# Three-block kernel with eight experts: 42 weight units multiplied whole in fp32, and a reordering of routing, row transposes and multiplications

## The chip, the cores and the metric

One Trainium2 chip, one core of it. The metric is the device time of one execution in microseconds (us). The kernel before was run three times: median 1424.33 us, from 1423.22 to 1425.75. The profile was taken of one more execution.

## What is computed

One sequence of 256 tokens with 1024 channels passes a gated-delta mixer, a SwiGLU block, a sliding-window attention block and a mixture of eight experts, each followed by a residual and a layer norm, all in fp32. The change lies in the last of them:

```python
def moe_swiglu(x, w_router, w_gate, w_up, w_down):
    bsz, t, d = x.shape
    xf = x.reshape(bsz * t, d)
    logits = (xf @ w_router).astype(jnp.float32)
    top_val, top_idx = lax.top_k(logits, TOP_K)
    top_w = jax.nn.softmax(top_val, axis=-1)
    gates = jnp.einsum('nk,nke->ne', top_w, jax.nn.one_hot(top_idx, N_EXPERTS, dtype=jnp.float32))
    out = jnp.zeros_like(xf)
    for e in range(N_EXPERTS):
        h = jax.nn.silu(xf @ w_gate[e]) * (xf @ w_up[e])
        out = out + gates[:, e:e + 1].astype(xf.dtype) * (h @ w_down[e])
    return out.reshape(bsz, t, d)
```

Each token takes two of the eight experts. Gate and up weights are 1024 x 3584 per expert, down weights 3584 x 1024: 44 MB of weights per expert, 352 MB in all.

## The kernel before, in words

**Units and the ring.** Expert weights arrive in units of 1 MB (128 partitions x 2048 fp32). An expert has 42: 14 for gate, 14 for up, 14 for down. SyncE (SP) issues their DMAs in the order of use, into a ring of ten tiles named `raw` (three of `ring_a`, two of `ring_m`, and five tiles of earlier stages); two of the ten leave the ring in the last expert, for the tiles `y` and `lngb`. A tile is free again once nothing reads it any more.

**Splitting.** `unit` (L141) makes two fp32r parts of a unit: `hi`, a cast on ScalarE (ACT, L154), and `lo = raw - hi`, a subtraction on VectorE (DVE, L155). Both have four buffers, so a split can be four units ahead of the multiplication.

**Heavy and light experts.** The rows of an expert's tokens, at most 128, are gathered to `xr`, transposed (L1139) and split into `xg` (high and low part). In `arms` (L1172) TensorE (PE) branches on the number of tokens. Above 64 the expert is *heavy*: `mm3` (L165) multiplies three times for each chunk of 128 channels and 512 columns (high x `hi`, low x `hi`, high x `lo`; L170, L171, L173). At or below 64 it is *light*: `packed` (L1109) has put 64 columns of the high part and 64 of the low part side by side into `xp`, and `mm2` (L1192) needs two products (L1195); `addlow` (L1184) then adds the lower half of the result to the upper one, by a product with `fold`. A unit has four chunk-and-column pairs, so it takes 12 products in a heavy expert and 8 in a light one. With the inputs used here the lines in the trace show experts 0, 2, 3 and 5 heavy, and 1, 4, 6 and 7 light. Expert 0 always takes the heavy path and gathers its rows by products (L1127) instead.

**The order of an expert.** Columns are taken in blocks `b` of 512, in pairs (0,1), (2,3), (4,5) and a single 6. The list `stages` runs, for a pair, gate of both, up of both, down of the *previous* pair, then a stage `held`. For a pair the even `b` holds channels 0 to 511 of both column blocks and the odd `b` channels 512 to 1023, two units each. `held` (from L1352) folds the up result and multiplies it with the activated gate: `V.tensor_mul(s_, s_, pu)` (L1355), tile `msg`. `turn_one` then transposes a `msg` (L1243) for the down products. `keep` stores an expert's result in `ys` at block 2 of the next expert.

**Routing.** After the last layer norm, `route` ranks the logits, `gates` (L1032) makes the softmax weights, and `places` (L1064) makes the row `key` of each token, on GpSimd (POOL) with reductions on DVE. Four indirect DMAs on POOL's queue (L1168) scatter the token rows to `xs`; `fetch` (L1117) loads one expert's rows to `xr`. `gather(e + 1)` is called behind the up stage of block 3 of expert `e`.

**Who sets the order.** The instructions of a stage are placed by a scheduler of the framework, not by the text alone; `tc.issue_after(i)` holds instructions back until `i` has been placed.

Of the kernel before, what the change touches and what calls it, by code (L numbers as in the profile page):

```python
# [30 lines left out]
P = 128  # L31
# [51 lines left out]
def kernel(ctx: ExitStack, tc: tile.TileContext, A, out):  # L83
# [73 lines left out]

    def colunits(w, c0, n):
# [8 lines left out]
    def mm3(ps, xh, xl, whs, first, last):  # L167
# [4 lines left out]
        for k, (_, wl) in enumerate(whs):  # L172
            PE.matmul(ps, xh(k), wl, start=False, stop=last and k == n - 1)  # L173
# [836 lines left out]
    def route(tb, plg, done):  # L1010
# [3 lines left out]
        gt_, eq_ = (rt.tile(sq, F32, name=n + str(tb)) for n in ("gt", "eq"))  # L1014
# [69 lines left out]
    with ExitStack() as mctx:  # L1084
# [36 lines left out]
        def gather(e):  # L1121
# [7 lines left out]

            if e == 0:  # L1130
                for k in range(KC):
                    pick(k, 0)
            for g in range(2):
                p = pg[g] if e == 0 else trb()
                for k in range(4 * g, 4 * g + 4):
                    if e == 0:
                        pick(k, 1)
                    else:
                        PE.transpose(p[:, k % 4 * P:(k % 4 + 1) * P], xr[e][:, k * P:(k + 1) * P], ident)  # L1139
# [7 lines left out]
        xg, xp = {}, {}  # L1147
# [14 lines left out]
        with tc.issue_after(placed.ins):  # L1162
            for tb in range(2):
                gates(tb, lgs[tb])
# [32 lines left out]
        def gateup(e, b, us, ps, then=lambda: None):  # L1197
# [4 lines left out]

            def parts():
# [284 lines left out]
```

## Time and profile before

| what | value |
|---|---|
| median of three runs | 1424.33 us |
| the profiled execution's own time | 1427.08 us |
| its span in the profile | 1425.4 us |
| PE, DVE, ACT busy | 1314.1, 1165.6, 1012.1 us |
| DMA bytes | 446.76 MB |
| first product of expert 0 | 475.2 us |

Each later expert is cut off where POOL stores the result of the one before it (the `ys` DMA, L1260): 634.80, 743.96, 868.56, 988.09, 1097.51, 1217.34 and 1325.01 us. Such a stretch begins in block 2 of an expert and ends in block 2 of the next, so it holds 34 units of one expert and 8 of the next.

How to read it: "busy" counts the time in which an engine has an instruction under way; PE's ends are modelled, so that its busy time also holds the drain of the last product before a gap. "Idle before" a group names what ended the wait. SPq, POOLq and PEq are the queues ahead of these engines. A PE product of fp32r operands has one record in the trace; one of fp32 operands has two.

### The profile page before, as it was taken

How to read it: one execution, taken by the hardware profiler on the slowest of the kernel's cores; microseconds unless marked ns; L12 is line 12 of the kernel's file. 1: busy time of each engine (PE TensorE's matmuls, PEld its weight loads, DVE VectorE, ACT ScalarE, POOL GpSimd, SP SyncE). 2: the span in 40 equal slices, each digit the busy share in tenths (PEclk: the TensorE clock that was granted, in tenths of full speed). 3: DMA queues.
4: the chain of work that ended last, by engine and by line, in shares of the span. 5: the costliest groups of instructions: out<-in, count | busy, mean ns of one | idle time of the engine just before them, and what ended most of it. 6: DMA issues, size and time to landing. Idle time of an engine off the chain costs nothing. (4 is left out here: it accounts for less than half of the span.)

```text
span 1425.4 us, 17392 instructions
## 1 busy us (share of the span) xinstructions
PE 1314.1 (92%) x6175; PEld 1046.2 (73%) x6175; DVE 1165.6 (82%) x1293; ACT 1012.1 (71%) x1264; POOL 68.0 (5%) x97
## 2 busy tenths in 40 slices
PE   7999999999898969988899999999889999888884
PEld 5888788888777858866677777776667777666663
DVE  4885975554878768889998887889999888999998
ACT  4764544443364657689888878779988888998983
POOL 4000000000000310000000000000000000002110
PEclk9999999999999889999999999999999999999997
DMA  8641577653644899999999999999999999999992
GB/s 283 208 125 60 178 271 237 229 207 120 226 148 170 307 366 336 362 368 392 419 413 380 367 358 368 376 343 408 413 420 411 377 369 374 396 414 416 419 416 87
DMA packets 145378, 446.76 MB, mean 313 GB/s; under 512 B 12704, under 2 KB 20032, under 8 KB 145264
## 3 DMA queue, kind: packets, MB, share of 16 engines
q1 hardware_dynamic: 137072, 420.64, 77.8%
q0 software_dynamic: 5280, 18.66, 3.5%
q10 hardware_dynamic: 2912, 5.90, 1.2%
q8 instruction: 76, 1.25, 0.3%
q14 instruction: 38, 0.31, 0.1%
HBM read 435.05 MB, written 15.36 MB: 316 GB/s over the span
## 5 line engine op out<-in xcount | busy, mean ns | idle before, releaser
L155 DVE TENSOR_TENSOR lo<-raw,hi 128x2048 fp32r<-128x2048 f32 (+1 forms) x610 | 910.3, 1532 | 119.1 <-ACT hi L154 109.2
L154 ACT CAST hi<-raw 128x2048 fp32r<-128x2048 f32 (+1 forms) x610 | 768.4, 1310 | 156.5 <-PE acc L171 61.3
L1195 PE MATMUL acc<-lo,xp 128*128 128x512 f32 x224 | 76.8, 431 | 22.3 <-DVE lo L155 20.1
L170 PE MATMUL acc<-hi,hT 128*128 128x512 f32 x224 | 89.1, 398 | 2.0 <-ACT hi L154 2.0
L170 PE MATMUL mm<-hi,xg 128*128 128x512 f32 x224 | 87.8, 393 | 0.5 <-ACT low L1189 0.5
L170 PE MATMUL acc<-hi,xg 128*128 128x512 f32 x224 | 87.8, 392 | 0.0
L171 PE MATMUL acc<-hi,hT 128*128 128x512 f32 x224 | 87.8, 392 | 0.0
L171 PE MATMUL mm<-hi,xg 128*128 128x512 f32 x224 | 87.4, 390 | 0.0
L171 PE MATMUL acc<-hi,xg 128*128 128x512 f32 x224 | 87.2, 389 | 0.0
L1195 PE MATMUL mm<-lo,xp 128*128 128x512 f32 x224 | 70.8, 403 | 9.6 <-DVE lo L155 9.4
L1195 PEld LDWEIGHTS acc<-lo,xp 128*128 128x128 f32 x224 | 39.6, 195 | 50.4 <-DVE lo L155 44.5
L1195 PE MATMUL acc<-lo,hp 128*128 128x512 f32 x224 | 71.5, 400 | 3.4 <-DVE lo L155 3.4
L1195 PE MATMUL acc<-hi,hp 128*128 128x512 f32 x224 | 70.8, 397 | 1.2 <-ACT hp L1115 1.2
L1195 PE MATMUL mm<-hi,xp 128*128 128x512 f32 x224 | 68.9, 394 | 2.2 <-ACT low L1189 1.5
L1195 PE MATMUL acc<-hi,xp 128*128 128x512 f32 x224 | 70.7, 403 | 0.0
L173 PE MATMUL acc<-lo,hT 128*128 128x512 f32 x224 | 69.4, 391 | 0.0
L173 PE MATMUL mm<-lo,xg 128*128 128x512 f32 x224 | 67.7, 389 | 0.0
L173 PE MATMUL acc<-lo,xg 128*128 128x512 f32 x224 | 67.7, 389 | 0.0
L1355 DVE TENSOR_TENSOR msg<-msg,acc 128x512 f32<-128x512 f32 x56 | 36.4, 681 | 36.5 <-PEq L1179 33.3
L1195 PEld LDWEIGHTS mm<-lo,xp 128*128 128x128 f32 x224 | 40.2, 188 | 26.8 <-DVE lo L155 19.4
L1114 ACT CAST hp<-tr 128x256 fp32r<-128x256 f32 x49 | 18.6, 380 | 54.7 <-DVE hT L1247 54.7
L1243 PE MATMUL tr<-ident,msg 128*128 128x128 f32 x224 | 34.9, 284 | 22.5 <-DVE msg L1355 22.5
(411 smaller groups left out, 2326.3 us busy)
## 6 DMA issues: line engine op xcount, KB each, us to landing
raw<-in_moe_w_gate_dram SPq DMA_DIRECT2D x112, 1024.0 KB, 7.6
raw<-in_moe_w_up_dram SPq DMA_DIRECT2D x112, 1024.0 KB, 7.5
raw<-in_moe_w_down_dram SPq DMA_DIRECT2D x112, 1024.0 KB, 7.9
raw<-in_a_w_in_dram SPq DMA_DIRECT2D x12, 1024.0 KB, 5.3
raw<-in_ffn_w_gate_dram SPq DMA_DIRECT2D x11, 1024.0 KB, 5.1
raw<-in_ffn_w_up_dram SPq DMA_DIRECT2D x11, 1024.0 KB, 5.0
raw<-in_ffn_w_down_dram SPq DMA_DIRECT2D x11, 1024.0 KB, 4.9
raw<-in_b_w_in_dram SPq DMA_DIRECT2D x5, 1024.0 KB, 5.0
```

Of the source, the lines that this page charges most:

```text
L154: S.copy(hi[:, c], raw[:, c])
L155: subs.append(V.tensor_sub(lo[:, c], raw[:, c], hi[:, c].bitcast(F32)))
L170: PE.matmul(ps, xh(k), wh, start=first and k == 0, stop=False)
L171: PE.matmul(ps, xl(k), wh, start=False, stop=False)
L173: PE.matmul(ps, xh(k), wl, start=False, stop=last and k == n - 1)
L1114: S.copy(v[:, :, 0], p)
L1195: PE.matmul(ps, x[:, (k0 + i % n) * P:(k0 + i % n + 1) * P], w, start=first and i == 0, stop=last and i == 2 * n - 1)
L1243: PE.transpose(p[:, f * P:(f + 1) * P], s[:, f * P:(f + 1) * P], ident)
L1355: V.tensor_mul(s_, s_, pu)
```

## The change

It does four things. (1) `as_is` loads a unit without splitting it. `loads` uses it in experts 1 to 7 for the second unit of the odd blocks 1, 3 and 5, of gate and of up (channels 768 to 1023): six units of an expert, 42 in all. `whole_part` multiplies such a unit directly, four products of fp32 operands for either path, with `xf`, a plain fp32 copy of the last two chunks of the transposed rows, which ACT makes once per expert. (2) `places` now runs ahead of `gates`, on DVE, and the scatters are issued ahead of `gates`; what weights the pairs is a function of its own, `pair_gates`. (3) `gather(1)` moves from block 3 to block 5 of expert 0, and its transposes are held until the products just recorded are placed. (4) The multiplication leaves `held` for the next pair's first gate stage, except behind blocks 5 and the last one.

```diff
+    def as_is(src, a, b):
+        raw = next(raws[0])()[:, :a * b].rearrange("p (a b) -> p a b", a=a)
+        nc.sync.dma_start(raw, src)
+        return raw
...
-            PE.matmul(ps, xh(k), wl, start=False, stop=last and k == n - 1)
+            turn[0] = PE.matmul(ps, xh(k), wl, start=False, stop=last and k == n - 1)
...
-        row, spill, one, val = (rt.tile(sq, F32, name=n) for n in ("row", "spill", "one", "val"))
-        G.tensor_tensor(row, pos, place[:, None, :E].to_broadcast(sq), op=OP.add)
-        G.tensor_tensor(spill, place[:, E:, None].to_broadcast(sq), row, op=OP.subtract)
-        G.tensor_scalar(val, pos, float(P), None, op0=OP.is_ge)
-        G.tensor_tensor(spill, spill, val, op=OP.mult)
-        G.tensor_tensor(row, row, spill, op=OP.add)
+        row, spill, val = (rt.tile(sq, F32, name=n) for n in ("row", "spill", "val"))
         key = rt.tile([P, 2, 2], F32, name="key")
+        V.tensor_tensor(row, pos, place[:, None, :E].to_broadcast(sq), op=OP.add)
+        V.tensor_tensor(spill, place[:, E:, None].to_broadcast(sq), row, op=OP.subtract)
+        V.scalar_tensor_tensor(spill, pos, float(P), spill, op0=OP.is_ge, op1=OP.mult)
+        V.tensor_add(row, row, spill)
         for j in range(2):
-            G.tensor_scalar(one, rank, float(j), None, op0=OP.is_equal)
-            for src, dst in ((row, key), (gate, gat2)):
-                G.tensor_tensor(val, one, src, op=OP.mult)
-                V.tensor_reduce(dst[:, j], val, axis=AX.X, op=OP.add)
-        V.tensor_copy(keyi, key)
+            V.scalar_tensor_tensor(val, rank, float(j), row, op0=OP.is_equal, op1=OP.mult)
+            V.tensor_reduce(key[:, j], val, axis=AX.X, op=OP.add)
+            V.tensor_copy(keyi[:, j], key[:, j])
...
+            late = ExitStack()
...
+            elif e == 1:
+                late.enter_context(tc.issue_after(turn[0].ins))
...
+                if g and e:
+                    xf[e] = mp.tile([P, 2 * P], F32, name="xf", tag="xf")
+                    S.copy(xf[e], p[:, 2 * P:])
...
         with tc.issue_after(placed.ins):
-            for tb in range(2):
-                gates(tb, lgs[tb])
             places()
...
+        with tc.issue_after(placed.ins):
+            for tb in range(2):
+                gates(tb, lgs[tb])
+            pair_gates()
...
+            def whole_part(ws):
+                for h, p in enumerate(ps):
+                    for k in range(2):
+                        PE.matmul(p, xf[e][:, k * P:(k + 1) * P], ws[:, k, h * 512:(h + 1) * 512], start=False, stop=k == 1)
...
                 for u, ws in enumerate(us):
+                    if not isinstance(ws, tuple):
+                        whole_part(ws)
+                        continue
...
-            return [unit(v[:, k0 + 2 * u:k0 + 2 * u + 2, c0:c0 + 1024], 2, 1024) for u in range(2)]
+            return [(as_is if e and k0 + 2 * u == KC - 2 else unit)(
+                v[:, k0 + 2 * u:k0 + 2 * u + 2, c0:c0 + 1024], 2, 1024) for u in range(2)]
...
+        def multiply():
+            for bb, pu, _, s_, ee in mine:
+                V.tensor_mul(s_, s_, pu)
+                held.append((ee, bb, s_))
+            mine.clear()
...
-                if held:
+                if b % 2 == 0 and b < NB - 1:
+                    multiply()
+                elif held:
                     turn_one()
...
-                if b == 3 and e + 1 < NE:
+                if b == 5 - 2 * (e > 0) and e + 1 < NE:
                     xg[e + 1] = gather(e + 1)
...
-                for bb, pu, _, s_ in mine:
-                    V.tensor_mul(s_, s_, pu)
-                    held.append((e, bb, s_))
-                mine.clear()
+                if b == NB - 2 or (e, b) == (NE - 1, NB - 1):
+                    multiply()
```

Where the scheduler puts this shows at three places. The first is PE in expert 0, behind the up products of block 3 (before) and of block 5 (now); `xr` holds the fetched rows of expert 1, `hT` the transposed `msg` for the down products, and `tr` is a PSUM bank. Before:

```order
1513 L170 MATMUL acc<-hi,xg 128x512
1514 L171 MATMUL acc<-hi,xg 128x512
1515 L173 MATMUL acc<-lo,xg 128x512 x2
1516 L1139 MATMUL tr<-ident,xr 128x128 x8
1517 L170 MATMUL acc<-hi,hT 128x512
```

Now, at the new place:

```order
1635 L175 MATMUL acc<-hi,xg 128x512
1636 L176 MATMUL acc<-hi,xg 128x512
1637 L178 MATMUL acc<-lo,xg 128x512 x2
1638 L1152 MATMUL tr<-ident,xr 128x128 x8
1639 L175 MATMUL acc<-hi,hT 128x512
```

The eight transposes moved back by 122 rows of PE's order, past the down products of blocks 0 and 1 and the gate and up products of blocks 4 and 5.

The second place is PE in a gate stage of an odd block of a later expert: the heavy path, a branch, the light path. `mm` is the gate's PSUM bank. Now:

```order
2703 L175 MATMUL mm<-hi,xg 128x512
2704 L176 MATMUL mm<-hi,xg 128x512
2705 L178 MATMUL mm<-lo,xg 128x512 x2
2706 L1224 MATMUL mm<-raw,xf 128x512 x4
2707 L1197 UNCONDITIONAL_BRANCH
2708 L1213 MATMUL mm<-hi,xp 128x512 x2
2709 L1213 MATMUL mm<-lo,xp 128x512 x2
2710 L1213 MATMUL mm<-hi,xp 128x512 x2
2711 L1213 MATMUL mm<-lo,xp 128x512 x2
2712 L1224 MATMUL mm<-raw,xf 128x512 x4
2713 L1197 UNCONDITIONAL_BRANCH
```

Before, the second half of either path was the first one over again; now four products read `raw` itself, in both paths.

The third place is DVE about the multiplications of a pair (`msg`), in expert 3. Before:

```order
721 L155 TENSOR_TENSOR lo<-raw,hi 128x2048
722 L1179 UNCONDITIONAL_BRANCH
723 L1355 TENSOR_TENSOR msg<-msg,acc 128x512 x2
724 L155 TENSOR_TENSOR lo<-raw,hi 128x2048
725 L1179 UNCONDITIONAL_BRANCH
726 L155 TENSOR_TENSOR lo<-raw,hi 128x2048
727 L1247 TENSOR_TENSOR hT<-tr,hT 128x512
```

Now:

```order
718 L155 TENSOR_TENSOR lo<-raw,hi 128x2048
719 L1197 UNCONDITIONAL_BRANCH
720 L1346 TENSOR_TENSOR msg<-msg,acc 128x512 x2
721 L155 TENSOR_TENSOR lo<-raw,hi 128x2048
722 L1197 UNCONDITIONAL_BRANCH
723 L155 TENSOR_TENSOR lo<-raw,hi 128x2048
724 L1273 TENSOR_TENSOR hT<-tr,hT 128x512
```

Between the down units' splits nothing moved: the multiplications stand where they stood, although the text calls them one stage later.

## Rows read from the trace of the kernel before

**Rows 1.** The page: span.

```profile
span 1425.4 us, 17392 instructions
```

**Rows 2.** Windows: stretches of experts 1, 2, 4 and 6, cut at the result DMAs.

```profile
core 0: us, PE busy (x) PEld busy (x) DVE busy (x) ACT busy (x) POOL busy (x), PEclk, DMA share, GB/s
634.80:744.00 109.20, 97.57 (x417) 73.00 (x416) 103.38 (x60) 99.29 (x98) 1.11 (x3) 1.00 1.02 408
744.00:868.60 124.60, 120.30 (x543) 98.19 (x542) 103.91 (x59) 99.84 (x95) 1.06 (x3) 1.00 0.97 367
988.10:1097.50 109.40, 97.69 (x416) 73.20 (x415) 103.35 (x59) 98.70 (x95) 1.06 (x2) 1.00 1.03 416
1217.30:1325.00 107.70, 93.80 (x388) 67.15 (x387) 104.22 (x59) 98.40 (x95) 8.98 (x7) 1.00 1.02 409
```

**Rows 3.** Timeline of PE in expert 0 (start, us, line, tiles, wait in brackets).

```profile
519.43 0.61 PE L173 MATMUL acc<-lo,xg 128*128 128x512 f32 x2
530.82 1.94 PE L1139 MATMUL tr<-ident,xr 128*128 128x128 f32 x8 [10.78 <-DMA xr<-xs]
```

**Rows 4.** Windows behind that wait; columns as in rows 2.

```profile
531.00:534.00 3.00, 3.00 (x12) 2.71 (x12) 1.28 (x2) 1.79 (x4) 0.55 (x1) 0.50 0.00 1
534.00:537.00 3.00, 3.00 (x12) 2.36 (x11) 2.52 (x6) 2.25 (x7) 0.00 (x0) 0.80 0.53 175
```

**Rows 5.** Timeline of POOL: the first scatter, the first fetch.

```profile
481.63 1.29 POOL L1168 DMA_INDIRECT xs<-x,keyi  x1 [0.58 <-DVE keyi L1079]
...
523.85 0.59 POOL L1119 DMA_DIRECT2D xr<-xs  x1 [7.31 <-issue]
```

**Rows 6.** Timeline of PE in expert 2, fp32r products.

```profile
774.76 0.39 PE L170 MATMUL mm<-hi,xg 128*128 128x512 f32 x1
...
777.48 0.39 PE L170 MATMUL mm<-hi,xg 128*128 128x512 f32 x1
```

**Rows 7.** Timeline of PE in the attention, fp32 products of 256 columns.

```profile
412.40 1.13 PE L890 MATMUL mm<-akT,aqT 64*128 64x256 f32 x4
413.46 0.50 PE L178 MATMUL acc<-hi,aTh 128*128 128x512 f32 x1
```

**Rows 8.** The same, fp32 products of 128 columns.

```profile
384.78 1.16 PE L890 MATMUL mm<-akT,aqT 64*128 64x128 f32 x8
385.86 0.39 PE L178 MATMUL mm<-hi,x2Th 128*128 128x256 f32 x1
```

**Rows 9.** Groups by form, stretch of expert 6 (busy us, mean ns, idle before).

```profile
L155 DVE TENSOR_TENSOR lo<-raw,hi 128x2048 fp32r<-128x2048 f32 x43 | 97.6, 2311 | 3.6 <-ACT hi L154 3.3
L154 ACT CAST hi<-raw 128x2048 fp32r<-128x2048 f32 x42 | 79.0, 1931 | 0.0
```

**Rows 10.** Timeline of PE in expert 2, about the transposes of a pair.

```profile
766.62 0.61 PE L173 MATMUL acc<-lo,hT 128*128 128x512 f32 x2
768.18 1.25 PE L1243 MATMUL tr<-ident,msg 128*128 128x128 f32 x8 [0.94 <-DVE msg L1355]
```

**Rows 11.** Waits of SP, same stretch (us in total, times, longest).

```profile
SPq L145 <- DVE lo L155: 89.7, 40, 4.5
```

**Rows 12.** DMA issues in that stretch (KB each, median us to landing).

```profile
raw<-in_moe_w_down_dram SPq DMA_DIRECT2D x13, 1024.0 KB, 8.0
```

**Rows 13.** Windows of 25 us in expert 7; columns as in rows 2.

```profile
1340.00:1365.00 25.00, 21.90 (x91) 15.44 (x90) 24.30 (x15) 22.42 (x21) 0.00 (x0) 1.00 1.02 420
```

**Rows 14.** DMA issues in expert 7, from 1335 to 1390 us.

```profile
raw<-in_moe_w_down_dram SPq DMA_DIRECT2D x10, 1024.0 KB, 13.2
```

**Rows 15.** Windows at the end; columns as in rows 2.

```profile
1390.00:1395.00 5.00, 5.00 (x18) 3.80 (x18) 5.00 (x7) 3.22 (x5) 0.00 (x0) 0.81 0.90 367
1400.00:1405.00 5.00, 3.83 (x17) 2.81 (x17) 5.00 (x4) 2.10 (x3) 0.00 (x0) 1.00 0.00 0
```

More of the change, by code (lines that the diff above doesn't have):

```diff
@@ L1013, in route @@
         sq = [P, E, E]
-        gt_, eq_ = (rt.tile(sq, F32, name=n + str(tb)) for n in ("gt", "eq"))
+        gt_, eq_ = (rt.tile(sq, F32, name=n, tag=n) for n in ("gt", "eq"))
         le, lo_ = lg[:, :, None].to_broadcast(sq), lg[:, None, :].to_broadcast(sq)
@@ L1066, in places, with pair_gates @@
         sq = [P, 2, E]
-        row, spill, one, val = (rt.tile(sq, F32, name=n) for n in ("row", "spill", "one", "val"))
-        G.tensor_tensor(row, pos, place[:, None, :E].to_broadcast(sq), op=OP.add)
-        G.tensor_tensor(spill, place[:, E:, None].to_broadcast(sq), row, op=OP.subtract)
-        G.tensor_scalar(val, pos, float(P), None, op0=OP.is_ge)
-        G.tensor_tensor(spill, spill, val, op=OP.mult)
-        G.tensor_tensor(row, row, spill, op=OP.add)
+        row, spill, val = (rt.tile(sq, F32, name=n) for n in ("row", "spill", "val"))
         key = rt.tile([P, 2, 2], F32, name="key")
+        V.tensor_tensor(row, pos, place[:, None, :E].to_broadcast(sq), op=OP.add)
+        V.tensor_tensor(spill, place[:, E:, None].to_broadcast(sq), row, op=OP.subtract)
+        V.scalar_tensor_tensor(spill, pos, float(P), spill, op0=OP.is_ge, op1=OP.mult)
+        V.tensor_add(row, row, spill)
         for j in range(2):
-            G.tensor_scalar(one, rank, float(j), None, op0=OP.is_equal)
-            for src, dst in ((row, key), (gate, gat2)):
-                G.tensor_tensor(val, one, src, op=OP.mult)
-                V.tensor_reduce(dst[:, j], val, axis=AX.X, op=OP.add)
-        V.tensor_copy(keyi, key)
+            V.scalar_tensor_tensor(val, rank, float(j), row, op0=OP.is_equal, op1=OP.mult)
+            V.tensor_reduce(key[:, j], val, axis=AX.X, op=OP.add)
+            V.tensor_copy(keyi[:, j], key[:, j])
+    def pair_gates():
+        val = rt.tile([P, 2, E], F32, name="gval")
+        for j in range(2):
+            G.tensor_scalar(val, rank, float(j), None, op0=OP.is_equal)
+            G.tensor_tensor(val, val, gate, op=OP.mult)
+            V.tensor_reduce(gat2[:, j], val, axis=AX.X, op=OP.add)
     def at(j, tb):
@@ L1132, in gather @@
                     pick(k, 0)
+            elif e == 1:
+                late.enter_context(tc.issue_after(turn[0].ins))
             for g in range(2):
                 p = pg[g] if e == 0 else trb()
[L1135 to L1139, printed above, removed]
+                with late.pop_all():
+                    for k in range(4 * g, 4 * g + 4):
+                        if e == 0:
+                            pick(k, 1)
+                        else:
+                            PE.transpose(p[:, k % 4 * P:(k % 4 + 1) * P], xr[e][:, k * P:(k + 1) * P], ident)
                 hi, lo = (xg[:, n, 4 * g:4 * g + 4, :].rearrange("p a c -> p (a c)") for n in range(2))
@@ L1345 @@
                         S.activation(s_, pg, AF.Silu)
-                        mine.append((b - len(pgs) + 1 + n, pu, low(pu) if e else None, s_))
+                        mine.append((b - len(pgs) + 1 + n, pu, low(pu) if e else None, s_, e))
                 if b == 1 and e + 1 < NE:
                     fetch(e + 1)
-                if b == 3 and e + 1 < NE:
+                if b == 5 - 2 * (e > 0) and e + 1 < NE:
                     xg[e + 1] = gather(e + 1)
@@ L1352 @@
                 if e:
-                    arms(e, lambda: None, lambda: [addlow(pu, lu_) for _, pu, lu_, _ in mine])
-                for bb, pu, _, s_ in mine:
-                    V.tensor_mul(s_, s_, pu)
-                    held.append((e, bb, s_))
-                mine.clear()
+                    arms(e, lambda: None, lambda: [addlow(pu, lu_) for _, pu, lu_, _, _ in mine])
+                if b == NB - 2 or (e, b) == (NE - 1, NB - 1):
+                    multiply()
                 if (e, b) == (NE - 1, NB - 1):
```

2 lines of the change are left out of this document (1 added, 1 removed).

## The prediction

> **What bounds the kernel now.** The page's span is 1425.4 us [rows 1]; the execution it shows took 1427.08 us, 2.75 us more than the median of the runs, 1424.33. The sum below is made against 1427.08 and its difference is then taken from the median. About 2.8 us, 0.2%, is what a measurement of this kernel can tell from no change.
>
> I read the expert stage by windows first, cut where an expert's result leaves. Two kinds of stretch appear [rows 2]. In heavy expert 2 PE is busy for 120.30 of 124.60 us, DVE and ACT for 104 and 100: PE is the bound. In light experts 1, 4 and 6 (109.2, 109.4, 107.7 us) DVE is busy for 103 to 104 us and PE for 94 to 98: DVE is the bound, with ACT (98 to 99) close behind. A share averaged over the kernel hides this: what helps a light expert, less splitting, costs a heavy one if PE has to do more.
>
> Data is not far off. DMA moves 408 to 416 GB/s in the light stretches [rows 2] and never much over the 420 GB/s of expert 7 [rows 13]. Still it is not what a light expert waits for: SP, which issues the loads, waits 40 times and 89.7 us for a subtraction of DVE to free a ring tile, and for nothing else [rows 11]. The ring thus runs full. Ten tiles of 2.56 us (107.7 / 42) are 25.6 us from issue to release; 8.0 us of that is the transfer [rows 12] and 4.2 us the cast and the subtraction (1.93 and 2.31 us, [rows 9]). So some 13 us, five tiles, lie landed and wait. In expert 7, with eight tiles, a transfer takes 13.2 us from issue to landing [rows 14] at 420 GB/s: there DMA is the bound, until the last load has landed at about 1395 us. From 1400 to 1405 us DVE is still busy throughout [rows 15].
>
> The one long wait of PE in this stage is in expert 0: 10.78 us at the transposes of expert 1's rows, for the fetch of `xr` [rows 3], which POOL could issue only at 523.85 us, behind four scatters, the first of them at 481.63 [rows 5]. The clock granted to PE is 0.50 in the 3 us behind it, the lower of its two levels (1.2 of 2.4 GHz), and 0.80 on average in the next three [rows 4]; ahead of that PE had stood for those 10.78 us.
>
> **The change part by part.**
>
> *Transposes later, keys first.* The order puts the eight transposes behind the up products of block 5. PE needs them there some 60 us later than now, and the rows come earlier, since nothing of the softmax stands ahead of the first scatter any more. The wait goes, 10.8 us, and so does the slow clock behind it: half of 3 us and a fifth of 3 us, 2.1 us. PE has no other idle time there that could swallow it. Gain 12.9 us; I allow 9 to 13, since the same eight transposes now delay the down products of block 2. What is late next is PE itself. The ten or so small instructions of the keys, moved from POOL to DVE, I take at nothing: DVE's splits are ahead of PE there, and without that cover they would cost some 2 us. `pair_gates` on POOL now stands between the first and the second scatter; nobody waits for those until block 5.
>
> *Whole units in the heavy experts 2, 3 and 5.* 18 units lose a cast and a subtraction, on engines that are not the bound: worth nothing. On PE twelve fp32r products leave: from 774.76 to 777.48 are twelve, 2.72 us [rows 6]. Four fp32 products of 512 columns come, eight records; no row has that shape. The nearest: four records of 256 columns take 1.06 us to the next product [rows 7], eight of 128 columns 1.08 us [rows 8]. Taking 2 columns' time at 2.4 GHz for each column, 0.107 and 0.213 us a record, both leave about 0.2 us that a group costs once. With 0.427 and 0.01 us a record and 0.19 a group, a unit takes 3.68 us, 0.96 more than now. Bounds: 3.41 us (no cost but the columns) and 4.20 us (0.525 a record, the straight line through the two rows). 18 units: **+17.3 us**, from +12.4 to +26.6. I take the middle value since it fits both rows.
>
> *Whole units in the light experts.* Each loses six casts and six subtractions: DVE falls from 104.2 to 90.3 us, ACT from 98.4 to about 87, one small copy for `xf` not counted. PE gains: now 336 products and 16 folds at 0.227 us and 36 transposes at 0.13 (eight are issued in 1.0 of the 1.25 us of [rows 10]) are 84.6 us; six units change 8 products (1.82 us) for 3.68, so +11.2. At each of four `held` stages PE also stands for 1.1 us, from 767.08, when the last product has been fed, to 768.18, when the first `msg` is there [rows 10]. Together 100.2 us: PE becomes the longest of the three. The gain of an expert is then at most 107.7 - 100.2 = 7.5 us. Data needs 42 units of 1.049 MB and 1.05 MB for rows and results, 45.1 MB; at 420 GB/s [rows 13] this is 107.4 us. A light expert can beat that only out of the tiles that lie ready: 7.2 us are three tiles of five. Experts 1 and 4 stand alone between heavy ones, in which the ring fills again (367 GB/s is all that expert 2 takes, [rows 2]). I take 5.5 us each, three quarters, because PE will meet a late split now and then; bounds 0 and 7.5.
>
> The Trainium skill ("DMA: Bandwidth & Descriptors", Specifications and "Where 436 GB/s comes from") speaks against any gain here: it says that loads from HBM are held to about 358 GB/s for a core, with 435 as the ceiling of the fabric. The rows stand at 408 to 420 and disagree with the first. By 358 a light expert would need an estimated 126 us and the terms of all light experts would be nought, the sum +4.4; by 435 data would need an estimated 103.7 us and those terms would reach the bounds of PE.
>
> *Experts 6 and 7* follow each other, so the tiles in hand count once. What DMA can still gain is the 409 of 420 GB/s of expert 6, 2.8 us, and at the end DVE, which works without a pause for some 10 us past the last landing, has fewer splits behind it: 2 us. One thing counts against: a whole unit holds its ring tile until PE has read it. I take 4 us; bounds 7 gained and 4 lost.
>
> *Multiplications later.* The order shows them on DVE where they were, and the transposes of `msg` on PE too, so the 1.1 us at each `held` stays. Nothing. Had they moved clear of that wait, seven experts could win 4.4 us each; the order excludes it.
>
> **Sum:** -12.9 + 17.3 - 5.5 - 5.5 - 4.0 = -10.6 us, 1416.5 us for the profiled execution and **1413.7 us** for the median.
>
> **The rivals.**
>
> *Dearer products.* The straight line of rows 7 and 8 holds: 4.20 us a unit, +26.6 in the heavy experts; in the light ones PE's sum rises to 103.3 and leaves 3, 3 and 2 us. -12.9 + 26.6 - 8 = +5.7: **1430 us.** For it: no row has 512 columns. Against: two lengths that nearly share a fixed rest.
>
> *The ring runs dry: slower.* Place: SP's queue, in order. A split frees its tile up to four units ahead of PE, a whole unit only behind it: in a light expert 4 x 2.56 us and the unit's 3.7 later. SP then stands, the loads under way (8.0 us, [rows 12]) run out, and DMA is idle for up to 4 us, six times an expert. In expert 2 there is room (367 of 420 GB/s). In light ones it decides as soon as the five landed tiles are used up: no gain in 1 and 4, and half of the 24 us lost in 6. -12.9 + 17.3 + 12 = +16.4: **1441 us.** Against: once PE waits for data, the splits are no longer four units ahead, and the pause shrinks below the 8 us that the loads under way cover.
>
> *Data bound at once.* The light experts fall to 107.4 us and no further: -2, -2 and -3. -2.6 us: **1421.7 us.** For it: 408 to 416 GB/s are near 420. Against: the five tiles. The HBM figure of the Trainium skill named above ("DMA: Bandwidth & Descriptors") is this case at its strongest, an estimated 1428.7 us; 408 to 420 GB/s speak against it.
>
> *Everything in hand is used.* 7.5 us in experts 1 and 4, 7 in the last two, a unit at 3.5 us (+14): -21.9, **1402.4 us.**
>
> **How the numbers follow.** Forecast 0.46, everything used 0.16, data bound 0.16, dearer products 0.11, ring dry 0.11. The forecast's own spread, from 14 to 20 us for the heavy units and 1.5 us either way for each light expert, leaves 0.03 of it within 2.8 us of no change; the data-bound case is split evenly between a small gain and none, the dearer one gives 0.02 to none. Faster 0.67, the same 0.13, slower 0.20. The range from 1400 to 1432 us leaves out the lower half of the best case and the dry ring.
>
> **What would show it.** No wait at the transposes of expert 1's rows, and expert 0's result 13 us earlier. The stretch of expert 2 at about 130 us, with PE busy throughout and eight fp32 records in 3.7 us. The stretches of experts 1 and 4 at about 104 us, with DVE near 90, and SP waiting for PE now at the tiles of whole units. The forecast is wrong if a light stretch stays at 107 us or more, if a whole unit takes 4 us, or if DMA shows gaps in expert 6.

## The result, and the profile of the changed kernel

The changed kernel takes 1440.61 us (median of four runs, 1438.31 to 1441.43) beside 1423.78 us for the kernel before in the same series: a ratio of 1.011, 95% interval 1.009 to 1.013. It is slower by 16.8 us; the forecast was faster by 10.6, and 1440.6 lies outside the range. The profiled execution took 1440.46 us with a span of 1438.7.

The windows of the four stretches that [rows 2] show, cut again where a result leaves (the columns are those of [rows 2]), and a window of expert 0:

```profile
618.00:733.60 115.60, 104.00 (x413) 72.27 (x412) 90.16 (x54) 89.45 (x92) 1.10 (x3) 1.00 0.99 390
733.60:863.70 130.10, 124.83 (x519) 93.74 (x518) 90.64 (x53) 89.62 (x90) 1.08 (x3) 1.00 0.92 356
988.70:1100.40 111.70, 103.25 (x409) 72.20 (x408) 90.26 (x53) 88.43 (x90) 1.02 (x2) 1.00 1.00 401
1225.70:1335.00 109.30, 99.29 (x389) 68.28 (x388) 91.19 (x53) 88.35 (x90) 10.63 (x7) 1.00 1.01 398
500.00:620.00 120.00, 117.95 (x525) 94.24 (x523) 101.58 (x71) 89.01 (x82) 2.94 (x4) 1.00 0.98 388
```

DVE's work in a light expert fell from 103 or 104 us to 90 or 91, as the prediction counted, yet no light stretch became shorter. Expert 0's result leaves 16.8 us earlier (618.04 us, before 634.80); everything behind it loses 30 us.

The timeline of PE (start, us, line, tiles, wait in brackets) answers [rows 3] and [rows 6]. The first three rows are a whole unit in heavy expert 2 and what follows it, the last three the same in expert 6:

```profile
752.77 3.59 PE L1224 MATMUL acc<-raw,xf 128*128 128x512 f32 x8
755.80 0.79 PE L175 MATMUL acc<-hi,hT 128*128 128x512 f32 x1
756.43 0.40 PE L176 MATMUL acc<-hi,hT 128*128 128x512 f32 x1
...
1240.27 3.59 PE L1224 MATMUL acc<-raw,xf 128*128 128x512 f32 x8
1243.30 1.03 PE L1203 MATMUL mm<-low,fold 128*128 128x512 f32 x2
1244.16 0.62 PE L1213 MATMUL acc<-hi,hp 128*128 128x512 f32 x2
```

A whole unit feeds for 3.03 us, and the products just behind it come 0.40 us late (0.63 us from 755.80 to 756.43, where a product otherwise takes 0.23). That is 3.43 to 3.44 us a unit, less than the 3.68 I took.

The waits in the stretch of expert 6 (us in total, times, longest); the last four rows answer [rows 11]:

```profile
ACT hp L1123 <- DVE hT L1273: 9.6, 5, 2.5
DVE msg L1346 <- PE acc L1203: 9.4, 3, 3.6
DVE lo L155 <- ACT hi L154: 8.3, 9, 2.5
PE mm L1213 <- DVE lo L155: 3.0, 5, 0.9
PE tr L1269 <- DVE msg L1346: 2.8, 4, 0.9
PE acc L1213 <- DVE lo L155: 2.7, 5, 0.7
SPq L145 <- DVE lo L155: 62.0, 21, 6.4
SPq L145 <- PE mm L1224: 10.5, 3, 4.7
SPq L145 <- PE mm L1203: 10.3, 2, 5.2
SPq L160 <- DVE lo L155: 5.0, 3, 2.4
```

DVE now stands 9.4 us at the multiplications until PE has done its fold, and 8.3 us for ACT's casts: what it saved, it waits away. PE still waits 5.7 us for subtractions (3.0 and 2.7). SP waits for PE too, but it still waits: the ring is full, and no cast in this stretch waits for a landing.

### The profile page after: what moved, and what is told of

Same layout as the page of the kernel before. It is cut to its first block, busy times and chain, and to the rows that moved or that the text cites. A ratio compares the mean times of both kernels' runs of the same rounds, so it can differ in the third digit from the quotient of the medians.

```text
span 1438.7 us, 17077 instructions
## 1 busy us (share of the span) xinstructions
PE 1348.7 (94%) x6103; PEld 1033.4 (72%) x6103; DVE 1074.3 (75%) x1258; ACT 941.3 (65%) x1229; POOL 69.2 (5%) x90
## 5 line engine op out<-in xcount | busy, mean ns | idle before, releaser
L155 DVE TENSOR_TENSOR lo<-raw,hi 128x512 fp32r<-128x512 f32 (+1 forms) x568 | 816.6, 1478 | 152.6 <-ACT hi L154 149.2
L154 ACT CAST hi<-raw 128x512 fp32r<-128x512 f32 (+1 forms) x568 | 689.2, 1260 | 154.8 <-PE acc L176 65.3
L175 PE MATMUL acc<-hi,hT 128*128 128x512 f32 x224 | 91.2, 407 | 0.0
L175 PE MATMUL acc<-hi,xg 128*128 128x512 f32 x188 | 77.3, 411 | 0.0
L1224 PE MATMUL mm<-raw,xf 128*128 128x512 f32 x168 | 75.5, 592 | 0.0
L1224 PE MATMUL acc<-raw,xf 128*128 128x512 f32 x168 | 75.5, 592 | 0.0
L175 PE MATMUL mm<-hi,xg 128*128 128x512 f32 x188 | 73.5, 392 | 0.5 <-ACT low L1207 0.5
L176 PE MATMUL mm<-hi,xg 128*128 128x512 f32 x188 | 73.3, 390 | 0.0
L176 PE MATMUL acc<-hi,xg 128*128 128x512 f32 x188 | 73.3, 390 | 0.0
L1380 ACT ACTIVATE msg<-mm 128x512 f32<-128x512 f32 x56 | 33.9, 606 | 55.4 <-PE acc L1224 33.4
L1213 PE MATMUL acc<-lo,xp 128*128 128x512 f32 x176 | 56.2, 408 | 11.5 <-DVE lo L155 10.8
L1213 PE MATMUL mm<-lo,xp 128*128 128x512 f32 x176 | 54.9, 400 | 6.9 <-DVE lo L155 6.9
L1213 PE MATMUL mm<-hi,xp 128*128 128x512 f32 x176 | 53.8, 394 | 2.1 <-ACT low L1207 1.4
```

What stands on the lines that cost most here:

```text
L154: S.copy(hi[:, c], raw[:, c])
L155: subs.append(V.tensor_sub(lo[:, c], raw[:, c], hi[:, c].bitcast(F32)))
L175: PE.matmul(ps, xh(k), wh, start=first and k == 0, stop=False)
L176: PE.matmul(ps, xl(k), wh, start=False, stop=False)
L1213: PE.matmul(ps, x[:, (k0 + i % n) * P:(k0 + i % n + 1) * P], w, start=first and i == 0, stop=last and i == 2 * n - 1)
L1224: PE.matmul(p, xf[e][:, k * P:(k + 1) * P], ws[:, k, h * 512:(h + 1) * 512], start=False, stop=k == 1)
```

## The experiments

Three theories were set against each other. *Queues in order*: ACT and DVE take their work in a fixed order, stand at the multiplication and its activation until PE comes, and cannot use the freed time. *Ring*: whole units hold their ring tiles until PE has read them, and data comes late. *Price*: PE's longer products alone. A period, below, runs from the first transpose of a pair's `msg` (blocks 2, 3) to that of the next pair (4, 5) in expert 6: 12 units and nothing else.

Stretches in us, from the one profiled execution of each kernel, each the difference of two issues of the result DMA; the last runs to the end of the span. The medians are of all runs; a kernel's ratio is to the kernel before in its own series:

| kernel | median | e1 | e2 | e3 | e4 | e5 | e6 | e7, end |
|---|---|---|---|---|---|---|---|---|
| before | 1423.8 to 1428.0 | 109.2 | 124.6 | 119.5 | 109.4 | 119.8 | 107.7 | 100.4 |
| change | 1440.61 | 115.5 | 130.1 | 125.0 | 111.8 | 125.3 | 109.3 | 103.7 |
| no_whole | 1413.83 | 107.5 | 124.6 | 119.5 | 109.4 | 119.8 | 107.7 | 102.9 |
| only_heavy | 1431.61 | 109.2 | 130.1 | 123.9 | 111.2 | 123.9 | 107.7 | 103.2 |
| only_light | 1424.42 | 114.1 | 124.6 | 120.9 | 110.2 | 121.2 | 109.5 | 103.9 |
| split_anyway | 1437.53 | 110.2 | 129.0 | 123.9 | 112.3 | 124.2 | 110.1 | 104.7 |
| after_fix | 1432.39 | 114.3 | 128.6 | 122.2 | 113.0 | 121.1 | 108.8 | 102.3 |
| early_fix | 1428.12 | 118.1 | 128.9 | 122.8 | 111.9 | 122.1 | 107.7 | 99.5 |
| nw_fix | 1410.19 | 110.1 | 124.3 | 118.6 | 110.7 | 118.6 | 107.6 | 99.3 |

**The parts one by one.**

```diff
-            return [(as_is if e and k0 + 2 * u == KC - 2 else unit)(
+            return [(unit)(                                                          # no_whole
+            return [(as_is if e in (2, 3, 5) and k0 + 2 * u == KC - 2 else unit)(     # only_heavy
+            return [(as_is if e in (1, 4, 6, 7) and k0 + 2 * u == KC - 2 else unit)(  # only_light
```

> The changed kernel with all 42 units of every expert split again; transposes later, keys first and multiplications later stay. Both theories (queues in order: DVE and ACT stand at the multiplications and lose the time freed; ring: whole units hold ring tiles until PE reads them) put the whole loss on the unsplit units, so both expect the 16.8 us that expert 0 gained to stay: 1407 to 1411 us, the stretches from expert 1 on within 1 us of the kernel before (109.2, 124.6, 119.5, 109.4, 119.8, 107.7). If the loss is in the moved pieces instead, 1420 us or more, with expert 1 at 113 us or more.

> Unsplit units only in experts 2, 3 and 5, where PE is the bound: both theories expect 5.5 us for each of the three, 16.5 us over the kernel without any unsplit unit, 1424 to 1427 us, and light experts 1, 4 and 6 as before at 109.2, 109.4 and 107.7 us.

> Unsplit units only in experts 1, 4, 6 and 7; the three heavy ones at 124.6, 119.5 and 119.8 us again. What I predicted before the result: 15 us gained in the light experts, 1393 to 1397 us. Queues in order: the light stretches stay at 111 to 115, 111 and 109 us, the last at 103.7, and the total is 1417 to 1423 us; DVE waits at the multiplications for PE, no engine waits for a landing. Ring: about the same total, but with DMA gaps and casts that wait for a landing.

Measured in one series with the kernel before at 1424.29 us: no_whole 1413.83, ratio 0.993 (0.991 to 0.995); only_heavy 1431.61, 1.005 (1.003 to 1.006); only_light 1424.42, 1.000 (0.998 to 1.001). So the moved pieces give 10.5 us, the 18 heavy units cost 17.8 and the 24 light ones cost 10.6. Together that is +17.9, and the change measures +16.8: the parts add up, and the light experts, from which 15 us were to come, are where the forecast fell. All three came out above the ranges that I had expected, by 3, 5 and 1 us: of the 16.8 us that expert 0 gained, not all stayed. By the stretches, 6.6 of the 13.7 us between the profiled executions of only_light and no_whole lie in expert 1. At its start ACT stands for a split buffer that PE is still reading, for 6.52 us in only_light (timeline of ACT):

```profile
611.93 1.91 ACT L154 CAST hi<-raw 128x2048 fp32r<-128x2048 f32 x1 [6.52 <-PE acc L176]
```

where in no_whole, which has a split more to do before, it is 3.60 us:

```profile
609.63 1.91 ACT L154 CAST hi<-raw 128x2048 fp32r<-128x2048 f32 x1 [3.60 <-PE acc L176]
```

Some 20 us later PE waits for late subtractions in the one (1.59 and 1.02 us) and not in the other. That the first leads to the second is read from the timelines and was not tested.

**What the moved multiplications do.**

```diff
-                if b % 2 == 0 and b < NB - 1:
-                    multiply()
-                elif held:
+                if held:
...
-                if b == NB - 2 or (e, b) == (NE - 1, NB - 1):
-                    multiply()
+                multiply()
```

> No unsplit unit and the multiplications at their old place in the program; what is left of the change is transposes later and keys first. The prediction took the moved multiplications at nothing: then as no_whole, 1411 to 1415 us. But expert 7's stretch was 102.9 us there against 100.4 before; if the moved multiplications cost that, 1409 to 1412 us and 100.4 us.

Without unsplit units, multiplications at their old place: 1413.15 us, ratio 0.993 (0.991 to 0.995). The same as no_whole: they are worth nothing. Expert 7 took 100.4 us, but expert 1 with its 109.4 us took that back.

**The freed time given back.** The casts and subtractions of the whole units are done all the same, and nobody reads them.

```diff
         nc.sync.dma_start(raw, src)
...
+        S.copy(hi, flat)
+        subs.append(V.tensor_sub(lo, flat, hi.bitcast(F32)))
         return raw
```

> The changed kernel, but the six units of an expert are still cast and subtracted, with nobody reading the result; DVE's order is that of the kernel without unsplit units. If the freed time of ACT and DVE were worth what I predicted, this costs the light experts the 11 us each of PE's added time on top of a DVE as busy as before: light stretches 115 us or more, total 1455 to 1470 us. If DVE's and ACT's freed time mostly goes into waits: light stretches at most 2 to 3 us over the change (111 to 114 us), total 1445 to 1453 us. Heavy stretches as in the change, 130 and 125 us, in either case.

1437.53 us, ratio 1.009 (1.006 to 1.011), beside 1.011 (1.009 to 1.013) for the change. Expert 6 takes 110.1 us with DVE busy for 104.4 of them, where the change takes 109.3 with 91.2 (columns as in [rows 2]):

```profile
1221.89:1332.03 110.14, 99.66 (x389) 68.10 (x388) 104.37 (x59) 99.15 (x96) 8.53 (x8) 1.00 1.00 395
```

Within a period the order of PE, DVE and ACT is that of the change, but for the two splits more. So thirteen us of DVE and eleven of ACT in each light expert are worth nothing that these runs can show; the total even lies under the 1445 us from which my ranges began. This is the shortest proof of the study. It also prices PE's part, since DVE's order is that of no_whole: by the two ratios some 22 us for the 42 units.

**PE's price taken away.** Whole units are multiplied as often as split ones, in fp32r, behind one fp32 product of two columns that reads the raw tile; their weights are left out of the sum. In the second kernel the multiplication, its activation and the low copies are pinned behind the split behind which the change has them.

```diff
+                PE.matmul(ps[0][:, 0:2], xf[e][:, 0:P], ws[:, 0, 0:2], start=False, stop=False)
...
-                        PE.matmul(p, xf[e][:, k * P:(k + 1) * P], ws[:, k, h * 512:(h + 1) * 512], start=False, stop=k == 1)
+                        for i in range(n):
+                            PE.matmul(p, xp[e][:, k * P:(k + 1) * P], xp[e][:, 512 * h:512 * (h + 1)],
+                                      start=False, stop=k == 1 and i == n - 1)
...
+            k = dlast[0] - 1                           # same_price_pin1
...
+                    queue(m, subs[k])
...
+                        queue(subs[k + 1], m)
```

> Each whole unit's eight fp32 records are replaced by as many fp32r products as a split unit has (8 light, 12 heavy, on the expert's packed rows as right side, so the weights of these units are left out of the sum), behind one fp32 product of two columns that reads the raw tile, so that the ring is held until PE comes. PE pays some 1.2 us less for each whole unit. Price theory: the light stretches fall to PE's 92 plus 6, 98 us, total 1390 us or less. Queues in order: DVE and ACT still stand and come late, light stretches 103 to 106 us, heavy 125 and 120, total 1400 to 1410 us. Ring theory: light stretches stay at 109 us or more, total 1420 us or more.

> The kernel in which whole units cost PE no more than split ones (their weights left out of the sum), with the multiplications pinned to where they stand in the changed kernel, one split later than the scheduler put them in same_price. Queues in order: that one place was what made it slow, so the light stretches fall from 113 to 117 us to 104 to 107, total 1402 to 1418 us. If instead the ring or something else of the whole units is at work, still 1440 us or more.

same_price takes 1454.66 us, ratio 1.022 (1.017 to 1.026): slower than the change, with less work on PE and as much on DVE and ACT. Its order has the multiplications one split earlier on DVE, behind the first down block instead of behind the first unit of the second. Pinned back by that one split it takes 1424.09 us, ratio 1.001 (0.999 to 1.002): 30.6 us less. The window of expert 6 (columns as in [rows 2]) and DVE's wait there at the multiplication, without the pin:

```profile
1231.93:1345.01 113.08, 94.72 (x400) 69.25 (x401) 91.18 (x52) 88.43 (x91) 9.31 (x7) 1.00 1.01 392
```

```profile
DVE msg L1349 <- PE acc L1203: 11.4, 3, 3.8
```

and with it:

```profile
1209.71:1317.85 108.14, 93.67 (x399) 68.90 (x398) 91.27 (x52) 88.37 (x90) 8.66 (x8) 1.00 1.02 410
```

```profile
DVE msg L1355 <- PE acc L1203: 5.5, 3, 3.7
```

A period (first transposes of two pairs, in the first kernel and then in the second) shows what the one place is worth by itself:

```profile
1253.90 1.25 PE L1272 MATMUL tr<-ident,msg 128*128 128x128 f32 x8 [0.62 <-DVE msg L1349]
1285.47 1.25 PE L1272 MATMUL tr<-ident,msg 128*128 128x128 f32 x8 [0.62 <-DVE msg L1349]
...
1230.36 1.25 PE L1272 MATMUL tr<-ident,msg 128*128 128x128 f32 x8 [0.68 <-DVE msg L1355]
1259.72 1.25 PE L1272 MATMUL tr<-ident,msg 128*128 128x128 f32 x8 [0.62 <-DVE msg L1355]
```

That is 31.6 and 29.4 us: 2.2 us, with PE's order the same and only the multiplications, their activations and the low copies moved on DVE and ACT. The 30.6 us are not all of that kind: at the first pair of an expert the pins also brought PE's transposes of `msg` ahead of the down products.

With the pin no engine is busy for more than 94 of 108.1 us, and still the stretch is no shorter than no_whole's 107.7 with DVE busy for 104. I had expected 104 to 107 there. So with load and price both taken away, the waits among the engines are left, and they hold the stretch where it was. Data is near, at 410 of 420 GB/s, but it does not hold it: no cast of expert 6 waits for a landing in no_whole, same_price_pin1 or early_fix (below).

**The ring and the split buffers.** ring8 takes two tiles out of the ring (`ring_m`); split5_ring8 makes a fifth pair of split buffers of them; the third does so without unsplit units.

```diff
-        turns = more_ring(mctx, "ring_m", 2, [raw_in(per, t) for t in ("Al", "Bl", "Ah")] + ylng)
+        turns = base + [raw_in(per, t) for t in ("Al", "Bl", "Ah")] + ylng
...
+        pairs[0] = cycle([split] * 4 + [fifth])       # split5_ring8
```

> The changed kernel with a ring of 8 raw tiles in place of 10 (6 in expert 7). Ring theory (whole units hold tiles, transfers start late): two tiles fewer are two transfers fewer under way, the light stretches grow by 4 us or more each, total over 1455 us. Queues in order: the ring has tiles to spare, stretches 1 to 6 within 1 us of 115.5, 130.1, 125.0, 111.8, 125.3, 109.3; only expert 7, with 6 tiles, may lose up to 6 us; 1439 to 1447 us.

> The changed kernel with a fifth pair of split buffers, for which the ring gives up two tiles (to be compared with the ring of 8 alone). Queues in order: ACT and DVE get one unit further ahead before they stand, so PE's waits for a subtraction in expert 6 (5.7 us) fall to 2 or less, the light stretches to 105 to 106 us and expert 1 to 110; some 15 us less than with the ring of 8 and four pairs. Ring theory: no less than with the ring of 8. Price of PE's products alone: within 3 us of the ring of 8.

> No unsplit unit, five pairs of split buffers, a ring of 8. DVE is busy for 104 of 107.7 us of a light stretch, so a longer lead has at most 3 us to give there: queues in order expects 1406 to 1416 us, no more than 2 us less for each light expert. If the ring matters, 1418 us or more.

ring8: 1444.30 us, ratio 1.013 (1.009 to 1.016), stretches 116.2, 130.1, 125.0, 111.9, 125.3, 109.8: within 0.7 us of the change. Only expert 7 loses 3.1, and its casts wait 6.5 us for landings; in expert 6 they wait 0.6. Two tiles less cost next to nothing in experts 1 to 6, where whole units hold tiles, so the ring theory falls there. The fifth pair gives nothing either: 1444.19 us, 1.013 (1.009 to 1.017), light stretches 112.2 and 109.8; the queue theory in its first form (the lead is capped by four buffers) falls with it. Without unsplit units: 1416.74, 0.994 (0.992 to 0.997).

**The place within a period.** The second of the four units of a pair is left whole in place of the last: PE's long product then lies just behind the multiplication. In the kernels with "fix", the multiplication goes back to `held`, the transposes of `msg` are issued there too, and the gate products of block 2 are tied behind them.

```diff
-            return [(as_is if e and k0 + 2 * u == KC - 2 else unit)(
+            return [(as_is if e and b % 2 == 0 and u == 1 else unit)(      # early_whole, early_fix
...
+                    if b == 2 and e and lastT[0] is not None:              # early_fix, after_fix, nw_fix
+                        cx.enter_context(tc.issue_after(lastT[0].ins))
```

> The same six unsplit units, but the second of the four of each gate and up pair of blocks (rows 256 to 511 of the weights) in place of the last: PE takes its long product just behind the multiplications, when DVE is late, instead of just ahead of them, when DVE has to stand. Queues in order: PE's waits for a subtraction (5.7 us in expert 6) and DVE's wait at the multiplications both shrink, the light stretches fall to 104 to 107 us, total 1420 to 1430 us. Ring: units hold their tiles as long as before, light stretches unchanged within 1 us, total 1438 to 1442 us. Price of PE's products alone: unchanged too.

> Whole units as second of four in each gate and up pair, PE's transposes tied ahead of the next gate products. If the place in the period decides (DVE sets the pace just behind the multiplications, PE ahead of them): light stretches 106 to 108.5 us, heavy as in the change, total 1428 to 1436 us. If PE's added time decides wherever it lies: light stretches 109 us or more, total 1438 us or more.

> The change with the same tie, as control: PE's order is nearly that of the change already, so within 3 us of it, 1437 to 1443 us.

> No unsplit unit, the same tie: 1410 to 1416 us, as no_whole.

early_whole: 1472.22 us, ratio 1.033 (1.030 to 1.036), 42 us over the range. The timelines at the border of experts 5 and 6 show why: the scheduler put the transposes of `msg` behind the gate products and a whole unit of block 2, ACT stood 5.27 us for them, and PE then 5.57 us for ACT at the next rows:

```profile
1250.40 0.59 ACT L1272 CAST hT<-tr 128x512 fp32r<-128x512 f32 x1 [5.27 <-PE tr L1269]
...
1249.77 1.04 PE L1269 MATMUL tr<-ident,msg 128*128 128x128 f32 x8
1256.37 1.12 PE L1152 MATMUL tr<-ident,xr 128*128 128x128 f32 x4 [5.57 <-ACT hp L1123]
```

Tied back, early_fix takes 1428.12 us, ratio 1.002 (1.001 to 1.003), against 1432.39, 1.006 (1.004 to 1.008), for its control after_fix, which is itself 8 us faster than the change where I expected 3 at most. The marks of a period, by the transposes of two pairs, for the change:

```profile
1249.03 1.25 PE L1269 MATMUL tr<-ident,msg 128*128 128x128 f32 x8 [0.63 <-DVE msg L1346]
1279.56 1.25 PE L1269 MATMUL tr<-ident,msg 128*128 128x128 f32 x8 [0.62 <-DVE msg L1346]
```

for split_anyway:

```profile
1245.74 1.26 PE L1274 MATMUL tr<-ident,msg 128*128 128x128 f32 x8 [0.67 <-DVE msg L1351]
1276.33 1.25 PE L1274 MATMUL tr<-ident,msg 128*128 128x128 f32 x8 [0.62 <-DVE msg L1351]
```

for after_fix:

```profile
1237.97 1.25 PE L1269 MATMUL tr<-ident,msg 128*128 128x128 f32 x8 [0.62 <-DVE msg L1346]
1268.54 1.25 PE L1269 MATMUL tr<-ident,msg 128*128 128x128 f32 x8 [0.62 <-DVE msg L1346]
```

for early_fix:

```profile
1241.04 1.25 PE L1269 MATMUL tr<-ident,msg 128*128 128x128 f32 x8 [0.69 <-DVE msg L1346]
1270.80 1.25 PE L1269 MATMUL tr<-ident,msg 128*128 128x128 f32 x8 [0.63 <-DVE msg L1346]
```

and for no_whole:

```profile
1223.38 1.25 PE L1269 MATMUL tr<-ident,msg 128*128 128x128 f32 x8 [0.67 <-DVE msg L1346]
1253.07 1.25 PE L1269 MATMUL tr<-ident,msg 128*128 128x128 f32 x8 [0.69 <-DVE msg L1346]
```

That is 30.5, 30.6, 30.6, 29.8 and 29.7 us; the kernel before has 29.7 too. With the whole units early, their added time on PE (2 x 1.6 us a period) is hidden all but 0.1 us; late, 0.8 to 0.9 us of it shows. Early or late, nothing is gained over 29.7. In total only expert 6, at 107.7 us, came into the 106 to 108.5 us that I had expected of light stretches: expert 1 is 3.8 us longer in early_fix than in after_fix, and why is open.

nw_fix, without unsplit units, is the fastest of the study: 1410.19 us, ratio 0.990 (0.988 to 0.991), 14 us faster than the kernel before and 30 faster than the change.

**Two waits moved, four misses.** msg_pin0 and nw_pin0 put the multiplications one split later on DVE and ACT, ht_pin and nw_ht_pin put DVE's part of `hT` one split earlier.

```diff
+            k = dlast[0] - 0                           # msg_pin0, nw_pin0; the rest as in same_price_pin1
...
+            if e and k < len(subs):                    # ht_pin, nw_ht_pin: the split `subs[k]` behind `ins`, DVE's part of hT
+                tc.add_manual_dep(subs[k].ins, ins.ins.name, mybir.DependencyInfo(...), reason="queue")
```

> The changed kernel with one thing pinned in the queues of DVE and ACT: the multiplications and what feeds them (activation, low copies) stand behind the split of the second unit of the second down block, one split later than now, and directly ahead of the next. Queues in order: DVE uses 2.3 of the 3.1 us for which it stands at each multiplication, PE's waits for a subtraction fall by half, PE's wait for the multiplication may grow by up to 0.5 us each; light stretches 106 to 108 us (now 109.3 to 111.8), heavy as now, total 1428 to 1436 us. Price of PE's products alone: within 2 us of the change, 1440 us.

> No unsplit unit, multiplications one split later by the same pins. Without unsplit units DVE never stands at a multiplication in a light expert, so the pin has nothing to use: queues in order expects PE's wait for the multiplications to grow by up to 2.3 us each and its waits for a subtraction to shrink as much, 1412 to 1420 us. A candidate for a version that beats both: only if under 1410 us.

> The changed kernel, with DVE's part of the turned rows (hT) pinned one split earlier on DVE, directly behind the split that follows the multiplications; PE's order in the light experts stays. ACT waits 9.6 us in expert 6 for that part of hT, DVE afterwards 8.3 us for ACT's casts, PE 5.7 us for subtractions. If that mutual wait of ACT and DVE carries the loss: ACT's wait falls under 4 us, PE's wait for subtractions to 2 or 3, light stretches 105 to 107, total 1425 to 1433 us. If PE's longer products alone carry it: light stretches within 1 us, 1438 to 1442 us.

> No unsplit unit, the same pins. DVE waits only 3.6 us for ACT's casts in a light stretch, so at most 3 us can be won in each: light 105 to 107.5 us, total 1404 to 1413 us. With under 1410 us it beats both kernels clearly.

1465.87, 1473.50, 1461.34 and 1440.30 us; ratios 1.030 (1.029 to 1.032), 1.035 (1.033 to 1.037), 1.023 (1.021 to 1.026) and 1.010 (1.007 to 1.013): all slower. In the first two PE's transposes followed the multiplications behind all four down units, and ACT then waits for them. In ht_pin ACT's wait for `hT` fell from 9.6 to 7.2 us and DVE's for the casts from 8.3 to 5.3, but DVE's wait at the multiplications grew from 9.4 to 12.8: the freed time moved on to the next stand. The period itself got 0.2 us shorter (30.3 for 30.5); what ht_pin lost lies ahead of it, between the transposes of an expert's first two pairs, where in expert 6's stretch PE waits 3.6 us for ACT at the transposes of `xr` (1.0 in the change).

## Why the prediction was wrong

The step that failed is "Whole units in the light experts": *PE becomes the longest of the three*, at 100.2 us, and *I take 5.5 us each, three quarters, because PE will meet a late split now and then*. With experts 6 and 7 this was to bring 15 us; only_light against no_whole shows a loss of 10.6 instead. PE did become the longest, but the stretch did not follow it. By the prediction's numbers for expert 6 a light stretch was to take 102.2 us: 95.8 of products and transposes, 4.4 at `held` and 2.0 for late splits. Expert 6 took 109.3: PE busy for 99.3, waiting 2.8 for `msg`, and idle for 7.2 more. Two terms were wrong.

First, the floor, by 3.5 us less the 1.6 that `held` fell short. I built PE's 84.6 us from products at their fastest pace, though [rows 2] had PE busy for 93.8 us in expert 6. From that row, with 3.44 - 1.82 = 1.62 us more for each of six units, PE would need 103.5 us. The run lies between the two counts, and with 99.3 + 2.8 = 102.1 us the floor alone would still have left the 5.5 us.

Second, the waits, by 5.2 us, the larger part. PE's idle time in the stretch had to fall from 13.9 us to 6.4; it fell to 10.0, 5.7 of it for subtractions. I treated these waits as a matter of DVE's load. The waits of PE for a subtraction in expert 6, before and in split_anyway:

```profile
PE acc L1195 <- DVE lo L155: 6.3, 9, 1.4
PE mm L1195 <- DVE lo L155: 3.6, 7, 0.9
...
PE acc L1218 <- DVE lo L155: 3.3, 5, 1.2
PE mm L1218 <- DVE lo L155: 3.0, 6, 0.9
```

They fell from 9.9 us before to 5.7 in the change, and to 6.3 in split_anyway, with DVE's load back. So it was PE's own slower pace that shortened most of them, not the freed splits. The timeline of DVE over one period of the change shows where the freed time lies:

```profile
1248.29 1.28 DVE L1346 TENSOR_TENSOR msg<-msg,acc 128x512 f32<-128x512 f32 x2 [2.88 <-PE acc L1203]
1249.49 4.49 DVE L155 TENSOR_TENSOR lo<-raw,hi 128x2048 fp32r<-128x2048 f32 x2
1253.89 0.69 DVE L1273 TENSOR_TENSOR hT<-tr,hT 128x512 fp32r<-128x512 f32 x1
1254.49 2.28 DVE L155 TENSOR_TENSOR lo<-raw,hi 128x2048 fp32r<-128x2048 f32 x1
1257.13 2.29 DVE L155 TENSOR_TENSOR lo<-raw,hi 128x2048 fp32r<-128x2048 f32 x1 [0.35 <-ACT hi L154]
1259.34 0.69 DVE L1273 TENSOR_TENSOR hT<-tr,hT 128x512 fp32r<-128x512 f32 x1
1262.56 13.30 DVE L155 TENSOR_TENSOR lo<-raw,hi 128x2048 fp32r<-128x2048 f32 x6 [2.54 <-ACT hi L154]
```

and of PE in its first part:

```profile
1256.83 0.73 PE L1213 MATMUL mm<-lo,xp 128*128 128x512 f32 x2 [0.59 <-DVE lo L155]
...
1259.47 0.73 PE L1213 MATMUL mm<-lo,xp 128*128 128x512 f32 x2 [0.53 <-DVE lo L155]
```

Behind the multiplications DVE works almost without a break and PE, with its 1.82 us a unit, waits for it twice. From 1261 us on PE has its whole units, DVE gets ahead in six splits in a row, and then stands at the next multiplications. The bound changes hands within each period, and the units that became cheaper for DVE lie in the part that PE sets. An average over the stretch (DVE 104 of 107.7) hides this, as one over the kernel hid the two kinds of expert. That the place counts is shown by early_fix (29.8 against 30.6 us a period in its control after_fix) and by the two same_price kernels (29.4 against 31.6). What keeps a period from falling clearly under 29.7 is not settled: with PE's long products gone as well it is 29.4 (same_price_pin1), taking part of ACT's and DVE's wait for each other out made 30.3 of 30.5 (ht_pin), and a multiplication moved later with PE's transposes kept in place was not tried in the change. Nor is the loss in expert 1 explained beyond what the timelines of only_light show.

The other steps:

- *Transposes later, keys first*, -12.9 us: held. The wait at the transposes of expert 1's rows [rows 3] is gone, PE is busy for 117.95 of 120 us from 500 us at a granted clock of 1.00 ([rows 4] had 0.50 and 0.80). Expert 0's result came 15.5 us earlier in no_whole, 16.8 in the change, and the kernel gained 10.5 by the medians (14.5 between the two profiled executions).
- *Whole units in the heavy experts*, +17.3: 17.8 measured; the sum is right in part by luck. The unit was cheaper than forecast (3.44 for 3.68 us, 13 us for 18 units); the other 4.8 us were not in the forecast. The windows show part of them: PE's idle time in the stretch of expert 2 grew from 4.3 to 5.3 us. With the transposes tied, after_fix loses less in heavy stretches (4.3, 3.6 and 2.5 us over nw_fix), so part of that rest seems to be order, not price.
- *Multiplications later*, nothing: right (old_mult).
- *The ring runs dry*, 1441 us: the rival that hit the number, by another way. Its place, SP waiting for PE, is in the profile, but no cast of expert 6 waits for a landing, and ring8 shows that tiles were to spare in experts 1 to 6. *Dearer products*: wrong, a unit costs less. *Data bound at once*: no; DMA fell to 398 GB/s in expert 6 while SP stood. The slices of the changed kernel's profile again reach 420 GB/s. The prediction quoted the Trainium skill ("DMA: Bandwidth & Descriptors") for 358 GB/s; under Measured that page gives some 358 to a core when both cores of the pair stream, and 425 at 16 MB to one core with the other idle. One core works here, and the 420 of this trace agree with the second figure, not with the first.
- The terms are linear to within 1.1 us (17.9 from the parts, 16.8 in the whole); not additivity but one term was wrong.
- One sum of the prediction is off: the terms of *Everything in hand is used* give -20.9 and 1403.4 us, not -21.9 and 1402.4. Nothing hangs on it.

## What to carry to other kernels

Before work is taken off the engine that looks busiest, follow one period of the steady state in time and note who waits for whom in each part: work removed where that engine is ahead is worth nothing. Set an engine's floor, counted from instructions at their fastest, beside its busy row, and add the waits that are there now until a run shows them gone. The cheapest test is to give the saved work back unused: if the time stays, that work was not the bound. And where a scheduler sets the order, compare every engine's order before reading an experiment: one place in the queues of DVE and ACT, with what it drew along, moved this kernel by 30 us, more than any part of the change.

## What the runs showed of the hardware

Four fp32 products of 512 columns feed in 3.03 us, 0.379 us a record, and delay the products behind them by some 0.40 us. One of two columns takes 0.14 us (from 704.94 to 705.08 us in same_price), and the twelve fp32r products behind it take 2.82 us, 0.1 more than twelve do in [rows 6]. So most of the delay comes with the long fp32 products, not with the change between the two kinds as such. The 0.427 us a record and 0.19 a group that I worked out of [rows 7, 8] were too much for the one and too little for the other; with the 0.01 a record they gave 1.08 and 1.12 us for the 1.06 and 1.08 of those rows, so the fit was not exact there either.
